# Encoder trunk: where TensorE's operands begin in SBUF, modulo 256 bytes

## The chip, the cores and the metric

One core of a Trainium2 chip runs the whole program. The metric is the device time of one execution in microseconds (us). SBUF is written here by the byte at which a tile begins in each of its 128 partitions; a tile's **residue** is that byte modulo 256.

## The reference

Two layers over 512 tokens of width 1024, and a memory of 256 tokens. Layer 0 mixes tokens by windowed attention, layer 1 by a bidirectional linear recurrence (RG-LRU); both also attend to the memory, and both end in a squared-ReLU MLP of width 4096:

```python
for l in range(DEPTH):
    h = rms_norm(x, mix_norm[l])
    kv = mem_n @ w_mem_kv[l]
    mixed, mq = attn_mixer(...) if l % 2 == 0 else lru_mixer(...)
    mo = memory_attention(mq, mk, mv)
    x = x + jnp.concatenate([mixed, mo], axis=-1) @ w_out[l]
    x = x + squared_relu_mlp(rms_norm(x, mlp_norm[l]), w_up[l], w_down[l])
return rms_norm(x, final_norm)
```

## The kernel before, in words

**Numbers.** Every product of float32 matrices is made of three matmuls in the type float32r. An operand is split into a high part (ScalarE, ACT, rounds it: `A.copy` or `A.activation`) and a low part (VectorE, DVE, subtracts), and TensorE (PE) adds high by high, high by low and low by high: `mm3`, lines 117 to 119, and in the MLPs lines 394 to 396. Each matmul has a **stationary** operand of 128 columns, which a weight load (PEld) brings in, and a **moving** operand of 256 or 512 columns, which streams past it. All data stands transposed: channels on partitions, tokens along the free dimension.

**Weights.** They come from HBM in 298 pieces of 128 x 1024 (512 KB) through tiles `raw` and are split into `wh` and `wl` (`split_w`, lines 112 and 113, outside the MLPs; `split_raw`, lines 351 and 352, in them). A tile `wh` holds eight stationary operands side by side.

**Stages, in the order of time.** The memory's keys and values of layer 0 (`ps_mk`, `ps_mv`); the memory attention (`ps_mq`, scores `sc` from `mq` and `mkh`, output `pv`); keys, values and queries (`ps_k`, `ps_v`, `ps_q`); window attention (`sc`, `pt`, `pv`); the output projection (`ps_o`, first from `om`, then from `o`, each 512 columns); MLP 0 from about 277 to 613 us; then the same for layer 1 with the recurrence (`ps_xb`, `ps_g`, `ps_gt`) in place of the window attention, and MLP 1 from 865 us to the end. Where the projections move tokens they move 512 columns (`h`, `om`, `o`, `ol`, `xh`); `ps_mk`, `ps_mv`, `ps_v` and the scores `sc` of the memory move 256.

**The MLPs** (`mlp`, line 425) cut each matrix product into 2 x 2 blocks and form it by seven block products (`seven`, line 399; `product`, line 386). Each block product is 24 matmuls that move 256 columns: `hx`, `h7` (activations of the up step) or `u7` (of the down step) move, `wh` and `wl` stand still. The last quarter of MLP 1's down step (`emit_last`, line 534) has plain products from `ul` into `ps_d`, 256 columns as well.

**What sets the order.** A scheduler orders the instructions by priority; `ahead(n)` raises it by n. The residues have no part in that.

**Where tiles lie.** Pools are stacks: those of the left side grow upward from byte 16,512 (residue 128), those with `side="right"` downward from byte 229,344. In a pool the tags lie in the order of their first tile, each tile rounded up to 32 bytes, with `bufs` of them side by side. So a pool's size shifts whatever is opened after it on its side. Lines that set residues before: the pad of 8 floats at line 73, the pools `const` (lines 77 to 82 and 613), `st` (lines 146 to 185), `mnm` and `msm` (286, 287), `nm`, `sm` and `dn` (745 to 747), `sink` (626), and the five tiles of line 827.

Of the kernel before, what the change touches and what calls it, by code (L numbers as in the profile page):

```python
# [9 lines left out]
F32 = mybir.dt.float32  # L10
# [13 lines left out]
NT = S // 128  # L24
# [8 lines left out]
C_FREQ, C_SIGN, C_HPI, C_END = 136, 137, 138, 139  # L33
# [26 lines left out]
def trunk(ctx: ExitStack, tc, xT_d, memT_d, wts_d, cols_d, ident_d, mask_d, pos_d, sink_d, outT_d, out_d, order):  # L60
# [6 lines left out]
    const = ctx.enter_context(tc.tile_pool(name="const", bufs=1))  # L67
    wp = ctx.enter_context(tc.tile_pool(name="wp", bufs=4))
    P = nc.gpsimd
    st = ctx.enter_context(tc.tile_pool(name="st", bufs=2))  # L70

    pad = ctx.enter_context(tc.tile_pool(name="pad", bufs=1, side="right"))
    pad.tile([128, 8], F32, name="pad")
    ps_m = ctx.enter_context(tc.tile_pool(name="ps_m", bufs=3, space=PSUM))
    ps_a = ctx.enter_context(tc.tile_pool(name="ps_a", bufs=2, space=PSUM))

    cols = const.tile([128, C_END], F32, name="cols")
    ident = const.tile([128, 128], F32, name="ident")
    ones = const.tile([128, 128], F32, name="ones")
    m_bc = const.tile([128, M], F32, name="m_bc")  # L80
    m_col = const.tile([128, 2], F32, name="m_col")
    xall = const.tile([128, KD, S], F32, name="xT")
    xT = [xall[:, c] for c in range(KD)]

# [79 lines left out]
    def rstd_cols(accs, n):  # L164
        nt = n // 128
        ps = ps_a.tile([128, S], F32, tag="pv", name="ps_ss", bufs=1)
        for t in range(nt):
            for i, acc in enumerate(accs):
                T.matmul(ps[:, t:t + 1], lhsT=acc[:, tok(t)], rhs=ones[:, 0:1], start=i == 0, stop=i == len(accs) - 1)
        v = st.tile([128, 4], F32, tag="v", name="v")[:, :nt]  # L170
        q = st.tile([128, 4], F32, tag="q", name="q")[:, :nt]
        r = st.tile([128, 4], F32, tag="r", name="r")[:, :nt]
        V.tensor_scalar(out=v, in0=ps[:, :nt], scalar1=1.0 / D, scalar2=EPS, op0=ALU.mult, op1=ALU.add)
        A.activation(out=q, in_=v, func=AF.Sqrt)
        V.reciprocal(out=r, in_=q)
        V.scalar_tensor_tensor(out=q, in0=r, scalar=-0.5, in1=r, op0=ALU.mult, op1=ALU.mult)
        V.tensor_tensor(out=q, in0=q, in1=v, op=ALU.mult)
        V.scalar_tensor_tensor(out=r, in0=q, scalar=1.5, in1=r, op0=ALU.add, op1=ALU.mult)
        return r
# [95 lines left out]
    def mem_attn(pool, w_in, col0, mkh, mvh, h, bc, o, bufs=2):  # L275
        for hd in range(4):
            ps = proj(load_w("s", w_in, col0 + hd * 128), h, "ps_mq")
            q = pool.tile([128, 2, S], F32R, tag="mq", name="mq", bufs=2)
            if bc is None:
                split_scaled(part(q), ps, 128.0 ** -0.5)  # L280
            else:
                qf = pool.tile([128, S], F32, tag="mqf", name="mqf", bufs=2)
                V.scalar_tensor_tensor(out=qf, in0=ps, scalar=128.0 ** -0.5, in1=bc, op0=ALU.mult, op1=ALU.mult)
                split(part(q), qf)
            p = pool.tile([128, NT, M], F32, tag="mp", name="mp", bufs=2)
            nm = pool.tile([128, NT], F32, tag="mnm", name="mnm", bufs=2)
            sm = pool.tile([128, NT], F32, tag="msm", name="msm", bufs=2)
            for g in range(2):
                sc = ps_a.tile([128, 2, M], F32, tag="sc", name="sc")
                for t2 in range(2):  # L290
                    mm3(sc[:, t2, :], part(q, tok(g * 2 + t2)), part(mkh[hd]), True, True)
                V.tensor_reduce(out=nm[:, g * 2:g * 2 + 2], in_=sc, axis=AX, op=ALU.max, negate=True)
                for t2 in range(2):
                    t = g * 2 + t2
                    A.activation(out=p[:, t, :], in_=sc[:, t2, :], func=AF.Exp, bias=nm[:, t:t + 1], scale=1.0,
                                 accum_out=sm[:, t:t + 1])
            V.reciprocal(out=sm, in_=sm)
            for t in range(NT):
                A.activation(out=p[:, t, :], in_=p[:, t, :], func=AF.Copy, scale=sm[:, t:t + 1])
            op = ps_a.tile([128, S], F32, tag="pv", name="pv", bufs=1)  # L300
            for m in range(2):
                pt = ps_a.tile([128, S], F32, tag="pt", name="pt")
                for t in range(NT):
                    T.transpose(pt[:, tok(t)], p[:, t, tok(m)], ident)
                ptr = pool.tile([128, 2, S], F32R, tag="mpt", name="mpt", bufs=2)
                split(part(ptr), pt)
                mm3(op, part(mvh[m], tok(hd)), part(ptr), m == 0, m == 1)
            split(part(o[hd]), op)
# [116 lines left out]
    def mlp(l, extra=None, extra2=None):  # L425
        hpm = tc.tile_pool(name=f"hm{l}", bufs=7, side="right")
        hm = hpm.__enter__()
        with tc.tile_pool(name=f"raws{l}", bufs=RAWS) as rp, tc.tile_pool(name=f"mlp{l}", bufs=2) as up:
            b = blocks_of(up)
            acc = st.tile([128, S], F32, tag="acc", name="acc", bufs=1)  # L430
            with ahead(AHEAD_E):
                plain = [hm.tile([128, 2, 4, 256], F32R, tag="h7", name="hx", bufs=7) for _ in range(2)]
            for c in range(KD):
                with ahead(AHEAD_E):
                    split_scaled(part(plain[c % 2], c // 2), xT[c][:, :256], col(C_MLP + 8 * l + c))
                add_square(acc, xT[c], c == 0)
# [97 lines left out]
            def emit_last():  # L534
                with tc.tile_pool(name="last", bufs=4, side="right") as lp:
                    u, b = {}, us.pop(3)
                    for n in (11, 21, 12, 22):
                        u[n] = lp.tile([128, 2, 4, 256], F32R, tag="ul", name="ul")
                        for k in range(2):
                            k = slice(2 * k, 2 * k + 2)  # L540
                            split((u[n][:, 0, k], u[n][:, 1, k]), b[n][:, k])

                    def down(w, half):
                        ps = mtile(256, "ps_d")
                        for k in range(KD):
                            mm3(ps, wcol(w, k), part(u[(11, 21)[k % 2] + half], k // 2), k == 0, k == KD - 1)
                        return ps

                    acc = st.tile([128, S], F32, tag="acc", name="acc", bufs=1)
                    for c in range(5):  # L550
                        w = load_w("s", f"w_down{l}", c * 128, 3 * 1024)
                        for half in range(2):
                            add_x(c, down(w, half), HALVES[half])
                        add_square(acc, xT[c], c == 0)
                    w = [load_w("s", f"w_down{l}", c * 128, 3 * 1024) for c in (5, 6, 7)]
                    for half in range(2):
                        cut = HALVES[half]
                        for c in (5, 6, 7):
                            add_x(c, down(w[c - 5], half), cut)
                            if half == 0 or c < 7:  # L560
                                add_square(acc[:, cut], xT[c][:, cut], False)
                        if half == 0:
                            final_first(acc, lp)
                    final_rest(acc, lp)
# [45 lines left out]


    nc.gpsimd.memset(ones, 1.0)
    warm = const.tile([128, 1], F32, name="warm")
    A.activation(out=warm, in_=ones[:, 0:1], func=AF.Sqrt)
    nc.sync.dma_start(out=cols, in_=cols_d)
    nc.scalar.dma_start(out=ident, in_=ident_d)
# [6 lines left out]
    at_a = tc.tile_pool(name="at_a", bufs=1, side="right")  # L623
    ap = at_a.__enter__()
    mask = ap.tile([128, 384], F32, name="mask")
    sink = ap.tile([128, 16], F32, name="sink")
    nsink = ap.tile([128, 16], F32, name="nsink")

    mkh, mvh = mkv_tiles(kv0)
    with tc.tile_pool(name="memp", bufs=1) as mp:  # L630
        fetched.append(fetch_w())
        raws, memH = load_mem(mp)
        fetched.append(fetch_w())
# [103 lines left out]
    def win_attn(g, pool, o):  # L737
        for n in range(NT):
# [4 lines left out]
            for ab in range(2):  # L743
                p = pool.tile([128, 4, 384], F32, tag="p", name="p", bufs=3)
                nm = pool.tile([128, 4], F32, tag="nm", name="nm", bufs=3)
                sm = pool.tile([128, 4], F32, tag="sm", name="sm", bufs=3)
                dn = pool.tile([128, 4], F32, tag="dn", name="dn", bufs=3)
                c0 = g * 8 + ab * 4
                for j in range(4):
                    sc = ps_a.tile([128, S], F32, tag="sc", name="sc")[:, :nk]  # L750
# [49 lines left out]
    def memory1():  # L800
        kv1 = mkv_pool.__enter__()
        mp = mem_pool.__enter__()
        mem1.extend([mkv_tiles(kv1), mp, fetch_mem(mp)])

    mlp(0, memory1, lambda: mem1.append(load_mem(*mem1[1:])[1]))
    (mkh, mvh), mp, _, memH = mem1
# [35 lines left out]
    V.tensor_tensor(out=ta, in0=ta, in1=sp4, op=ALU.add)  # L842
    V.tensor_scalar(out=sp4, in0=ta, scalar1=4.0, scalar2=None, op0=ALU.mult)
    V.tensor_scalar(out=sp8, in0=ta, scalar1=-8.0, scalar2=None, op0=ALU.mult)

    rt, it, tt, xcs, xhs, hs, o_l = {}, {}, {}, {}, {}, {}, {}

# [151 lines left out]
```

## Time and profile before

| | us |
|---|---|
| median of three runs (1198.85, 1205.08, 1212.76) | 1205.08 |
| the profiled execution's own time | 1205.16 |
| its span, from first to last instruction | 1203.4 |
| PE busy with matmuls | 1157.5 |
| DVE busy | 1013.7 |
| ACT busy | 767.2 |

The span and the time differ by 1.8 us, which lie around the first and last instruction. A matmul's length in the trace (0.28 us for 256 columns) runs from its start to the end of its results and overlaps the next one's; what counts for the time is the **period**, from one start to the next. A stretch of back-to-back matmuls of one form gives it: its length divided by their number, less two that had begun before the stretch and are counted in it.

### The profile page before, as it was taken

To read this page: it belongs to the slowest core of one execution; us is meant where nothing else is said; L and a number is where in the kernel's file an instruction comes from. 1 tells how busy PE (TensorE), PEld (TensorE's weight loads), DVE (VectorE), ACT (ScalarE), POOL (GpSimd) and SP (SyncE) were. 2 spreads that over 40 slices of the span, in tenths; PEclk is the share of its full clock that TensorE was granted. 3 is DMA by queue.
4 is the path that set the end of the run, shared out by engine and by line. 5 is a ranking of instruction groups with operands and counts; after the bars stand their busy time and mean duration, and the time that the engine had idled before them with its cause. 6 is when DMAs were issued, how large, how long until landed. Compare 5 with 4: busy or idle time off the path is not lost.

```text
span 1203.4 us, 20324 instructions
## 1 busy us (share of the span) xinstructions
PE 1157.5 (96%) x8084; PEld 1065.1 (89%) x8084; DVE 1013.7 (84%) x1464; ACT 767.2 (64%) x1194; POOL 53.3 (4%) x69
## 2 busy tenths in 40 slices
PE   6999999997999999999989999999969999999997
PEld 6888788886999999999988877777869999999997
DVE  6978899868988969859978679998799798896964
ACT  7685488844666565566446779983547755757632
POOL 0000000000010101010000000001001000010000
PEclk9999999999999999999989999999989999999999
DMA  7412201162476875785434122228217766687232
GB/s 247 158 54 88 88 19 36 53 209 71 136 206 159 218 210 156 191 215 162 103 121 141 53 88 88 89 104 244 71 53 193 211 180 201 163 227 210 72 106 70
DMA packets 48910, 164.44 MB, mean 137 GB/s; under 512 B 5552, under 2 KB 9008, under 8 KB 48816
## 3 DMA queue, kind: packets, MB, share of 16 engines
q1 hardware_dynamic: 39456, 130.90, 31.3%
q0 software_dynamic: 8640, 31.46, 14.5%
q8 instruction: 63, 1.03, 0.3%
q10 hardware_dynamic: 720, 0.79, 0.2%
q14 instruction: 31, 0.25, 0.1%
HBM read 161.04 MB, written 2.10 MB: 136 GB/s over the span
## 4 chain that ended last, share of the span: by engine, by line
PE 75%; DVE 17%; ACT 3%; DMA 3%; issue 2%; SPq 0%; DVEq 0%; ACTq 0%
PE ps L395 13%; PE ps L394 13%; PE ps L396 13%; DVE wl L352 3%; PE ps_o L117 3%; PE ps_o L119 3%; PE ps_o L118 3%; DMA raw<-wts 2%; DVE xT L528 2%; PE sc L752 2%; PE pt L772 1%; DVE wl L113 1%; PE pv L117 1%; PE ps_mq L118 1%; PE ps_q L119 1%
## 5 line engine op out<-in xcount | busy, mean ns | idle before, releaser
L351 ACT CAST wh<-raw 128x1024 fp32r<-128x1024 f32 x210 | 219.1, 1048 | 178.1 <-PE ps L395 120.7
L352 DVE TENSOR_TENSOR wl<-raw,wh 128x1024 fp32r<-128x1024 f32 x210 | 254.9, 1217 | 60.5 <-ACT wh L351 59.7
L394 PE MATMUL ps<-h,wh 128*128 128x256 f32 x832 | 234.3, 282 | 12.1 <-ACT h L134 12.1
L395 PE MATMUL ps<-h,wh 128*128 128x256 f32 x832 | 234.4, 282 | 6.3 <-DVE h L135 6.3
L396 PE MATMUL ps<-h,wl 128*128 128x256 f32 x832 | 233.7, 281 | 0.0
L396 PE MATMUL ps<-u,wl 128*128 128x256 f32 x784 | 218.9, 279 | 1.9 <-DVE wl L352 1.8
L394 PE MATMUL ps<-u,wh 128*128 128x256 f32 x784 | 219.3, 280 | 1.1 <-DVE xT L528 1.0
L395 PE MATMUL ps<-u,wh 128*128 128x256 f32 x784 | 218.7, 279 | 0.6 <-DVE u L135 0.6
L394 PEld LDWEIGHTS ps<-h,wh 128*128 128x128 f32 x832 | 158.7, 191 | 12.7 <-ACT h L134 12.5
L395 PEld LDWEIGHTS ps<-h,wh 128*128 128x128 f32 x832 | 158.4, 190 | 7.3 <-DVE h L135 7.3
L396 PEld LDWEIGHTS ps<-h,wl 128*128 128x128 f32 x832 | 160.2, 192 | 0.0
L396 PEld LDWEIGHTS ps<-u,wl 128*128 128x128 f32 x784 | 149.1, 190 | 2.3 <-DVE wl L352 2.3
L394 PEld LDWEIGHTS ps<-u,wh 128*128 128x128 f32 x784 | 148.0, 189 | 2.0 <-issue 1.7
L395 PEld LDWEIGHTS ps<-u,wh 128*128 128x128 f32 x784 | 147.9, 189 | 0.8 <-DVE u L135 0.8
L112 ACT CAST wh<-raw 128x1024 fp32r<-128x1024 f32 x88 | 92.0, 1047 | 62.8 <-DMA raw<-wts 32.2
L113 DVE TENSOR_TENSOR wl<-raw,wh 128x1024 fp32r<-128x1024 f32 x88 | 106.9, 1216 | 28.8 <-ACT wh L112 28.5
L328 POOL DMA_DIRECT2D raw<-wts x60 | 51.9, 865 | 1061.5 <-DMA raw<-wts 487.1
L345 DVE TENSOR_TENSOR raw<-raw 128x1024 f32<-128x1024 f32 x60 | 73.0, 1219 | 0.8
L528 DVE TENSOR_TENSOR xT<-xT,ps 128x512 f32<-128x512 f32 x98 | 65.7, 676 | 0.8 <-PE ps L396 0.8
L134 ACT CAST u<-b 128x1024 fp32r<-128x1024 f32 x42 | 43.9, 1049 | 14.3 <-PE ps L396 8.3
L135 DVE TENSOR_TENSOR u<-b,u 128x1024 fp32r<-128x1024 f32 x42 | 50.9, 1212 | 0.0
L217 DVE TENSOR_TENSOR xT<-xT,ps_o 128x512 f32<-128x512 f32 x48 | 32.6, 679 | 7.8 <-PE ps_o L119 7.5
(284 smaller groups left out, 2644.2 us busy)
## 6 DMA issues: line engine op xcount, KB each, us to landing
raw<-wts SPq DMA_DIRECT2D x238, 512.0 KB, 4.2
raw<-wts POOLq DMA_DIRECT2D x60, 512.0 KB, 7.4
mraw<-memT SPq DMA_DIRECT2D x16, 128.0 KB, 4.5
xT<-xT SPq DMA_DIRECT2D x8, 256.0 KB, 5.1
outT<-xT SPq DMA_DIRECT2D x8, 128.0 KB, 1.8
out<-fo ACTq DMA_DIRECT2D x2, 256.0 KB, 3.0
out<-fo SPq DMA_DIRECT2D x2, 256.0 KB, 3.1
posi<-pos SPq DMA_DIRECT2D x1, 256.0 KB, 5.4
```

The costliest lines, as they stand in the source:

```text
L112: A.copy(out=h, in_=raw)
L113: V.tensor_tensor(out=l, in0=raw, in1=h.bitcast(F32), op=ALU.subtract)
L117: T.matmul(out, lhsT=lhsT[0], rhs=rhs[0], start=start, stop=False)
L135: V.tensor_tensor(out=dst[1], in0=src, in1=dst[0].bitcast(F32), op=ALU.subtract)
L328: P.dma_start(out=t, in_=wts_d[fetch_n[0]], accum_op=ALU.add)
L345: V.tensor_tensor(out=a["s"], in0=a["s"], in1=a[22 if i == 6 else 12], op=ALU.add)
L351: A.copy(out=h, in_=raw)
L352: V.tensor_tensor(out=l, in0=raw, in1=h.bitcast(F32), op=ALU.subtract)
L394: T.matmul(out, lhsT=wh[:, c], rhs=t[:, 0, k], start=first, stop=False, skip_group_check=True)
L395: T.matmul(out, lhsT=wh[:, c], rhs=t[:, 1, k], start=False, stop=False, skip_group_check=True)
L396: T.matmul(out, lhsT=wl[:, c], rhs=t[:, 0, k], start=False, stop=p == 1 and k == 3, skip_group_check=True)
L528: V.tensor_tensor(out=dst, in0=dst, in1=src, op=ALU.add if n < 20 else ALU.subtract)
```

## The change

It computes nothing else, and no instruction is added or taken out: it adds tiles that nobody uses and makes small tiles wider, so that other tiles begin elsewhere. The tile `warm` moves ahead of `xT`.

```diff
-    pad.tile([128, 8], F32, name="pad")
+    pad.tile([128, 56], F32, name="pad")
...
-    cols = const.tile([128, C_END], F32, name="cols")
+    cols = const.tile([128, 160], F32, name="cols")[:, :C_END]
...
-    m_col = const.tile([128, 2], F32, name="m_col")
+    m_col = const.tile([128, 64], F32, name="m_col")[:, :2]
+    warm = const.tile([128, 64], F32, name="warm")[:, :1]
...
-        r = st.tile([128, 4], F32, tag="r", name="r")[:, :nt]
+        r = st.tile([128, 12], F32, tag="r", name="r")[:, :nt]
...
-            nm = pool.tile([128, NT], F32, tag="mnm", name="mnm", bufs=2)
-            sm = pool.tile([128, NT], F32, tag="msm", name="msm", bufs=2)
+            nm = pool.tile([128, 16], F32, tag="mnm", name="mnm", bufs=2)[:, :NT]
+            sm = pool.tile([128, 16], F32, tag="msm", name="msm", bufs=2)[:, :NT]
...
         with tc.tile_pool(name=f"raws{l}", bufs=RAWS) as rp, tc.tile_pool(name=f"mlp{l}", bufs=2) as up:
+            up.tile([128, 32], F32, tag="pad", name="pad", bufs=1)
...
                 plain = [hm.tile([128, 2, 4, 256], F32R, tag="h7", name="hx", bufs=7) for _ in range(2)]
+                hm.tile([128, 32], F32, tag="pad", name="pad", bufs=1)
...
                             split((u[n][:, 0, k], u[n][:, 1, k]), b[n][:, k])
+
+                    lp.tile([128, 32], F32, tag="pad", name="pad", bufs=1)
...
-    warm = const.tile([128, 1], F32, name="warm")
...
-    sink = ap.tile([128, 16], F32, name="sink")
+    sink = ap.tile([128, 48], F32, name="sink")[:, :16]
...
     with tc.tile_pool(name="memp", bufs=1) as mp:
+        mp.tile([128, 32], F32, tag="pad", name="pad", bufs=1)
...
                 dn = pool.tile([128, 4], F32, tag="dn", name="dn", bufs=3)
+                if n == 0 and ab == 0:
+                    pool.tile([128, 56], F32, tag="pad", name="pad", bufs=1)
...
         mem1.extend([mkv_tiles(kv1), mp, fetch_mem(mp)])
+        mp.tile([128, 32], F32, tag="pad", name="pad", bufs=1)
...
     V.tensor_scalar(out=sp8, in0=ta, scalar1=-8.0, scalar2=None, op0=ALU.mult)
+
+    lp.tile([128, 48], F32, name="pad", bufs=1)
```

Added up by the rule above, the tiles that TensorE reads have these residues:

| tiles | part in the matmul | before | after |
|---|---|---|---|
| `wh`, `wl` | stationary; moving in `ps_mv` and `ps_v` | 0 | 0 |
| `hx`, `h7`, `u7`, `ul` (both MLPs) | moving, 256 columns | 192 | 128 |
| `h`, `om`, `ol` | moving, 512 columns (`h` stationary in `ps_v`) | 192 | 0 |
| `o` (window attention) | moving, 512 columns | 64 | 0 |
| `xh` | moving, 512 columns | 0 | 0 |
| `memH` | moving, 256 columns, in `ps_mk`; stationary in `ps_mv` | 192 | 128 in layer 0, 0 in layer 1 |
| `mkh`, `k` | moving, 256 and 256 or 384 columns | 192 | 0 |
| `mq`; `q` | stationary | 192; 64 | 0 |
| `mvh`, `v` | stationary | 192 | 0 |
| `mpt`; `ptr` | moving, 512 columns | 64; 224 | 0 |

The steps from one operand to the next inside a tile (512, 1024, 2048 or 4096 bytes) are multiples of 256, so a whole tile has one residue. In layer 1's pool `memp1` the pad comes between the tiles `mraw` (then at 128) and `memH`. In the MLPs the left pools then end at byte 171,648, where the right ones begin; 1,024 bytes were free between them before.

## Rows read from the trace of the kernel before

**Rows 1.** The page's parts 1 and 4: engines' busy time, and the chain that ended last.

```profile
span 1203.4 us, 20324 instructions
PE 1157.5 (96%) x8084; PEld 1065.1 (89%) x8084; DVE 1013.7 (84%) x1464; ACT 767.2 (64%) x1194; POOL 53.3 (4%) x69
...
PE 75%; DVE 17%; ACT 3%; DMA 3%; issue 2%; SPq 0%; DVEq 0%; ACTq 0%
```

**Rows 2.** Costliest groups, shapes apart: 256-column matmuls of the MLPs; idle time stands last.

```profile
L395 PE MATMUL ps<-h,wh 128*128 128x256 f32 x832 | 234.4, 282 | 6.3 <-DVE h L135 6.3
L394 PE MATMUL ps<-h,wh 128*128 128x256 f32 x832 | 234.3, 282 | 12.1 <-ACT h L134 12.1
L396 PE MATMUL ps<-h,wl 128*128 128x256 f32 x832 | 233.7, 281 | 0.0
L394 PE MATMUL ps<-u,wh 128*128 128x256 f32 x784 | 219.3, 280 | 1.1 <-DVE xT L528 1.0
...
L117 PE MATMUL ps_d<-ul,wh 128*128 128x256 f32 x128 | 35.4, 277 | 0.0
...
L394 PE MATMUL ps<-hx,wh 128*128 128x256 f32 x64 | 18.0, 282 | 0.0
```

**Rows 3.** Stretches of the two MLPs: length, then each engine's busy time and instructions.

```profile
core 0: us, PE busy (x) PEld busy (x) DVE busy (x) ACT busy (x) POOL busy (x), PEclk, DMA share, GB/s
317.50:548.50 231.00, 231.00 (x1963) 231.00 (x1963) 193.09 (x197) 147.04 (x187) 20.72 (x24) 1.00 0.70 190
549.00:555.00 6.00, 4.18 (x22) 3.90 (x21) 6.00 (x7) 3.81 (x5) 0.00 (x0) 0.74 0.51 167
555.50:594.00 38.50, 38.02 (x333) 37.77 (x332) 38.50 (x41) 21.10 (x21) 3.45 (x4) 1.00 0.66 177
889.80:899.00 9.20, 9.20 (x80) 9.20 (x80) 8.64 (x10) 6.95 (x8) 0.00 (x0) 1.00 0.17 57
899.50:907.00 7.50, 5.07 (x30) 5.03 (x30) 7.35 (x9) 1.92 (x3) 0.00 (x0) 0.77 0.23 75
907.00:985.00 78.00, 78.00 (x691) 78.00 (x690) 70.11 (x72) 56.17 (x72) 6.91 (x8) 1.00 0.75 205
990.00:1060.00 70.00, 70.00 (x620) 70.00 (x619) 60.43 (x61) 44.65 (x54) 5.17 (x6) 1.00 0.70 195
...
1150.00:1185.00 35.00, 35.00 (x311) 35.00 (x311) 16.25 (x27) 11.43 (x18) 0.00 (x0) 1.00 0.18 61
```

**Rows 4.** Stretches of 512-column matmuls: ps_q, ps_o from o, ps_o from ol.

```profile
105.00:143.00 38.00, 38.00 (x165) 30.45 (x164) 33.66 (x53) 14.78 (x19) 0.00 (x0) 1.00 0.27 98
252.00:277.00 25.00, 25.00 (x111) 20.52 (x110) 17.66 (x26) 11.16 (x18) 3.60 (x4) 1.00 0.99 286
828.00:865.00 37.00, 37.00 (x161) 29.79 (x160) 25.64 (x37) 14.97 (x23) 1.73 (x2) 1.00 0.57 165
```

**Rows 5.** Timeline of PE, ps_g from 788.63 us: start, length, engine, line.

```profile
788.63 0.40 PE L117 MATMUL ps_g<-xh,wh 128*128 128x512 f32 x1
...
790.69 0.39 PE L117 MATMUL ps_g<-xh,wh 128*128 128x512 f32 x1
```

**Rows 6.** Timeline of PE, memory scores sc from 66.97 us: twelve in a row.

```profile
66.97 0.28 PE L117 MATMUL sc<-mkh,mq 128*128 128x256 f32 x1
...
68.27 0.28 PE L119 MATMUL sc<-mkh,mq 128*128 128x256 f32 x1
```

**Rows 7.** Timeline of PE, ps_mv of layer 1, thirteen in a row.

```profile
631.07 0.28 PE L118 MATMUL ps_mv<-wl,memH 128*128 128x256 f32 x1
...
632.43 0.28 PE L118 MATMUL ps_mv<-wl,memH 128*128 128x256 f32 x1
```

**Rows 8.** Stretch of ps_v, 256 columns.

```profile
88.10:99.40 11.30, 11.30 (x98) 11.30 (x97) 10.46 (x19) 8.07 (x16) 0.00 (x0) 1.00 0.14 47
```

**Rows 9.** Costliest groups: DVE's splits of weights, raw of L352 at residue 192, L113 at 0.

```profile
L352 DVE TENSOR_TENSOR wl<-raw,wh 128x1024 fp32r<-128x1024 f32 x210 | 254.9, 1217 | 60.5 <-ACT wh L351 59.7 <-DMA raw<-wts 0.5
...
L113 DVE TENSOR_TENSOR wl<-raw,wh 128x1024 fp32r<-128x1024 f32 x88 | 106.9, 1216 | 28.8 <-ACT wh L112 28.5
```

## The prediction

> **What bounds the kernel now.** I read the page first, then the groups by shape, then stretches of one kind of matmul. The page has PE busy for 96% of the span and 75% of the chain that ended last; DVE holds 17% of that chain [rows 1]. The idle time before the MLPs' matmuls is small: 12.1 and 6.3 us ahead of the h products and hardly any ahead of the others, against more than 200 us of busy time in each group [rows 2]. So in most of the span the time is a number of matmuls times their period.
>
> The period is not one number. Between 317.5 and 548.5 us the 256-column matmuls follow each other at 231.0 us / 1,961 = 117.8 ns. From 907 us on it is 78.0 / 689 = 113.2, then 70.0 / 618 = 113.3, and in the last products of MLP 1 35.0 / 309 = 113.3 [rows 3]. The granted clock is 1.00 (the level of 2.4 GHz) in all of these, the residues are the same (stationary 0, moving 192), and neither the group of weights nor h or u makes a difference. So there are two levels, 4.5 ns apart, and a run of matmuls stays in one of them. The level changes where PE stood idle: between 549 and 555 us it was busy for 4.18 of 6.00 us and the clock fell (mean 0.74), and between 899.5 and 907 us again (5.07 of 7.50 us, 0.77); before each the period was slow (9.2 / 78 = 117.9 ns just before the second), and after the second it was fast [rows 3]. Right after the first, at 555.5 to 594 us, DVE is busy throughout and sets the pace.
>
> The 512-column matmuls differ with the residue that moves. At 192 the period is 38.0 / 163 = 233.1 ns in `ps_q` and 37.0 / 159 = 232.7 in `ps_o` from `ol`; at 64, in `ps_o` from `o`, the same code on other tiles, it is 25.0 / 109 = 229.4 [rows 4]. At 0, in `ps_g`, nine periods take 2.06 us, 228.9 each [rows 5]. I read this as two streams of reads, the moving operand's and the next weight load's, that cost each other time depending on where each stands.
>
> **The change part by part.** No instruction is added, removed or moved to another queue, no wait is added, and the DMAs are the same in number and size. What can change is the duration of what reads or writes a tile that begins elsewhere.
>
> *DVE and ACT.* The same split of a weight takes 1,217 ns where `raw` is at residue 192 (L352) and 1,216 where it is at 0 (L113) [rows 9]. These engines' durations don't depend on it: nothing.
>
> *512 columns, moving residue 192 to 0.* Projections are 34 with 24 matmuls (816), output projections at 192 make 384: 1,200 matmuls. Ends: 0, if the residue is only a companion of something else in `ps_q`; or 233.1 less two fast 256-column periods, 226.6: 6.5 ns x 1,200 = 7.8 us. I take the row with the very residues of the change, 228.9 [rows 5], which `ps_o` at 64 supports [rows 4]: 4.2 ns. About 1,000 of the 1,200 stand in back-to-back runs as in [rows 4], where PE sets the pace (DVE is busy there for 33.66 of 38.00 us at most, so it keeps up with a PE 2% faster); the rest lie between waits, where I count nothing. 4.2 ns x 1,000 = 4.2 us less. The 192 of `ps_o` from `o` go from 64 to 0: 0.5 ns x 192 = 0.1 us, nothing.
>
> *256 columns in the MLPs, moving residue 192 to 128.* These are 2,496 with h, 2,352 with u, 192 with hx and 384 with ul [rows 2]: 5,424. No row shows a moving residue of 128. What rows show around it: residues of equal size (192 and 192, the memory's scores) take 1.30 us for eleven periods, 118.2 [rows 6]; stationary 192 with moving 0 has both levels, 12 periods in 1.36 us = 113.3 in `ps_mv` [rows 7] and 11.3 / 96 = 117.7 in `ps_v` [rows 8]. So a distance of 64 or 192 between the two allows both levels and a distance of 0 is near the slow one. Ends: all 5,424 at 118.2, or all at 113.3. Of the 5,424, 1,961 + 78 = 2,039 are shown at the slow level [rows 3]; I take the rest, 3,385, as fast. All fast: 2,039 x 4.5 = 9.2 us less. All at 118.2: 3,385 x 4.9 + 2,039 x 0.4 = 17.4 us more. I take the lower end. A distance of 128 is half of the 256 bytes, so the two streams stand as far apart as residues allow. That this leaves only the fast level is an assumption; the nearest evidence is that the slower periods above belong to distances 0, 64 and 192. What is late next: in the fast stretches DVE is busy for 70.11 of 78.00 us and 60.43 of 70.00 [rows 3] and PE still has no gap, so nothing else takes over; only in the DVE-bound 38.5 us after 555.5 us can a faster PE gain nothing, and no slow matmuls are counted there.
>
> *The other 256-column groups* (`ps_mk`, `ps_mv`, `ps_v`, the memory's scores) are short and change pairs of residues; `ps_mv` and `ps_v` together are 288 matmuls, 288 x 4.5 = 1.3 us either way. I take zero.
>
> *The full SBUF.* Left and right pools meet in the MLPs where 1,024 bytes were free. They still don't overlap, so no tile waits for another that it did not wait for. Zero.
>
> Sum: 1205.16 (the profiled execution, within 0.1 us of the median) - 4.2 - 9.2 = 1191.8 us.
>
> A rule of the Trainium skill speaks against any effect. Its page "TensorE: Matmul & The Clock Gate", Part 2, has TensorE read the moving operand and the weights through two independent ports of SBUF, so that loading the next weights takes nothing from the running matmul, with N / 2.4 + 2.5 ns between matmuls (109.2 for 256 columns, 215.8 for 512); and "SBUF — State Buffer", section Operand start alignment, asks only for a multiple of the element size. Then residues would change nothing. The trace disagrees: 229.4 against 233.1 ns at two residues [rows 4], and both are above that figure.
>
> **The rivals.**
>
> 1. *Both levels stay at 128.* The level would again be drawn where PE has stood idle, and only the 512-column part gains: 1205.2 - 4.2 = 1201.0 us, with up to 8.8 us (the long slow run, 1,961 x 4.5 ns) to either side by the draw. For it: both levels are seen at distance 64 and at 192 alike [rows 3, 7, 8], and the spread of the three runs, 13.9 us, is of the size of one such long run. Against: nothing is seen at 128.
>
> 2. *Slower: the MLPs lose the fast level.* If 128 puts the weight load and the moving operand in each other's way for good, as the equal residues do [rows 6], every MLP matmul takes about 118.2 ns: 1205.2 + 17.4 - 4.2 = 1218.4 us. It decides as soon as the MLPs' mean period rises by more than 4.2 us / 5,424 = 0.8 ns. For it: the fast level depends on how two streams interlock, and that can be lost as well as won; over half of the MLPs' matmuls are fast already. Against: even the equal residues cost hardly more than the slow level.
>
> 3. *No effect.* The 4 ns between `ps_q` and `ps_o` from `o` come from elsewhere, and the change does not do what it says: 1205.2 us. For it: the difference of levels within one pair of residues shows that something other than the residue sets 4.5 ns. Against: three separate 512-column groups order themselves by residue.
>
> The rule of two independent ports comes out as rival 3.
>
> **How the numbers follow.** Chances: forecast 0.45, rival 1 0.30, rival 2 0.15, rival 3 0.07, and 0.03 for periods below 113.3 that no row shows. Faster by over 1% means under 1193.0, slower by over 1% means over 1217.1 (about what a measurement of this kernel can tell from no change). The forecast lies 1.2 us inside the first bound and falls short of it about once in six: 0.45 x 0.83 = 0.37; rival 1 reaches it with a good draw, 0.05; the last case 0.03: faster 0.45. Rival 2 is over the upper bound half of the time, and an unlucky draw of rival 1 or more cost than 118.2 adds a little: slower 0.12. Within 1%: 0.43. The range goes from 1184 (all 512-column matmuls at 226.6 and the short groups gaining too: 1205.2 - 7.8 - 9.2 - 1.3 = 1186.9, and a little for fewer waits) to 1214 (rival 1 with its worst draw is 1209.8, and rival 2 at the slow level of 117.8 only, 3,385 x 4.5 = 15.2 us more, 1216.2; the range takes in the first and stops short of the second). The likeliest case alone would be 1187 to 1196.
>
> **What would show it.** In the profile after, stretches such as 317 to 548 us must have 113.3 ns in both MLPs, over at least 95% of their back-to-back matmuls, and no long run at 117.8. `ps_q` and `ps_o` must come down from 233 to about 229 ns. Idle time of PE must stay as it is. The prediction is wrong if long runs at 117.8 or above remain in an MLP (rivals 1 and 2, told apart by whether 113.3 is still found), if the 512-column periods stay at 233 (rival 3), or if DVE's share in the chain grows by as much as PE's falls.

## The result, and the profile after

The kernel with the change takes 1213.7 us (median of 12 runs, 1209.2 to 1217.8) against 1202.5 us before (12 runs, 1198.9 to 1212.8): the ratio is 1.008, with an interval of 1.0055 to 1.0106. It is slower by 0.8%, where 1191.8 us had been forecast. The profiled execution took 1213.68 us, 8.5 us more than the one of before.

The page of the kernel after, parts 1 and 4:

```profile
span 1211.9 us, 20324 instructions
PE 1166.9 (96%) x8084; PEld 1081.5 (89%) x8084; DVE 1015.7 (84%) x1464; ACT 767.8 (63%) x1194; POOL 53.3 (4%) x69
...
PE 75%; DVE 16%; DMA 3%; ACT 3%; issue 2%; SPq 0%; DVEq 0%; ACTq 0%
```

Against [rows 1] the number of instructions is the same and PE's busy time is 9.4 us longer; the span grew by 8.5 us, so PE's idle time did not grow. The time went into the matmuls themselves. The stretches of the kernel after, first four of the MLPs, then `ps_q`, `ps_o` from `o`, `ps_o` from `ol`, and `ps_v` (columns as in [rows 3]; line numbers are two to eleven higher after the change):

```profile
318.00:550.00 232.00, 232.00 (x1957) 232.00 (x1956) 191.78 (x195) 147.61 (x187) 20.71 (x24) 1.00 0.69 189
567.00:608.00 41.00, 41.00 (x348) 41.00 (x347) 41.00 (x48) 20.21 (x20) 1.72 (x2) 1.00 0.45 122
990.00:1060.00 70.00, 70.00 (x592) 70.00 (x592) 57.30 (x57) 42.72 (x53) 5.17 (x6) 1.00 0.67 181
1157.00:1193.00 36.00, 36.00 (x306) 36.00 (x305) 14.59 (x24) 10.39 (x17) 0.00 (x0) 1.00 0.16 57
99.00:141.50 42.50, 42.50 (x189) 35.15 (x188) 37.43 (x59) 16.68 (x23) 0.00 (x0) 1.00 0.29 100
250.00:275.00 25.00, 25.00 (x112) 20.71 (x111) 17.28 (x25) 10.72 (x18) 3.60 (x4) 1.00 0.96 289
825.00:862.00 37.00, 37.00 (x165) 30.61 (x164) 26.40 (x38) 15.36 (x24) 1.72 (x2) 1.00 0.60 168
87.10:98.60 11.50, 11.50 (x98) 11.50 (x97) 10.60 (x20) 8.29 (x16) 0.00 (x0) 1.00 0.13 46
```

In MLP 0 the period is 232.0 / 1,955 = 118.7 ns, in MLP 1 it is 70.0 / 590 = 118.6 and in its last products 36.0 / 304 = 118.4. Both levels of [rows 3] are gone from the long stretches, and what took their place is slower than either. The row of 990 us is the plainest to read: the same 70 us held 620 matmuls before and hold 592 now, at a granted clock of 1.00 both times. The 512-column matmuls became faster, and more than forecast: 42.5 / 187 = 227.3 ns in `ps_q`, 25.0 / 110 = 227.3 and 37.0 / 163 = 227.0 in `ps_o`, against 233.1, 229.4 and 232.7 [rows 4]. Length over count can be off by one matmul, which is 1 to 2 ns in stretches as short as these. From the first start to the last of the same rows of matmuls the periods are 226.8, 226.7 and 227.0 after, and 233.3, 228.9 and 233.3 before.

The sum by these rows, with the prediction's counts: 3,385 matmuls of the MLPs rose from 113.3 to 118.7 ns, 2,039 from 117.8 to 118.7: 18.3 + 1.8 = 20.1 us more. Of the 512-column matmuls 1,200 fell by about 6.5 ns, 7.8 us less, and 192 by 2.2 ns, 0.4 us less. That makes 11.9 us more, against 11.2 between the medians and 8.5 between the two profiled executions. The agreement hides two terms that are too large. Both kernels run the same 8,084 matmuls in the same order, so the start of one and the same matmul can be compared in the two traces:

| from the first matmul of a stage to that of the next, us | before | after | after less before |
|---|---|---|---|
| start of the program to MLP 0 | 277.50 | 275.54 | -1.96 |
| MLP 0 | 335.89 | 339.53 | +3.64 |
| layer 1, `ps_mk` | 17.56 | 14.31 | -3.25 |
| layer 1, from `ps_mv` to MLP 1 | 234.48 | 232.75 | -1.73 |
| MLP 1 to the end | 337.95 | 349.77 | +11.82 |

The MLPs cost 15.5 us more and not 20.1. The stages with 512 columns gave 3.7 us and not 8.2, in part because waits took up some of it: from `ps_mv` to MLP 1 PE is idle for 5.7 us after and for 3.7 before. The 3.3 us in `ps_mk` are no gain of the change: there PE waited for 2.45 us in the execution of before, and the granted clock fell (mean 0.81), while after it waited for 1.65 us and the clock stayed at 1.00. The kernel before_mlp128 below has the old residues in this stage and took 12.49 us, at 1.00. Before and after:

```profile
613.40:631.00 17.60, 15.15 (x107) 14.95 (x106) 11.89 (x21) 8.33 (x14) 0.00 (x0) 0.81 0.45 149
615.10:629.30 14.20, 12.55 (x106) 12.34 (x105) 11.66 (x21) 8.05 (x14) 0.00 (x0) 1.00 0.41 144
```

### The profile page after: what moved, and what is told of

Same layout as the page of the kernel before. It is cut to its first block, busy times and chain, and to the rows that moved or that the text cites. A ratio compares the mean times of both kernels' runs of the same rounds, so it can differ in the third digit from the quotient of the medians.

```text
span 1211.9 us, 20324 instructions
## 1 busy us (share of the span) xinstructions
PE 1166.9 (96%) x8084; PEld 1081.5 (89%) x8084; DVE 1015.7 (84%) x1464; ACT 767.8 (63%) x1194; POOL 53.3 (4%) x69
## 4 chain that ended last, share of the span: by engine, by line
PE 75%; DVE 16%; DMA 3%; ACT 3%; issue 2%; SPq 0%; DVEq 0%; ACTq 0%
PE ps L397 15%; PE ps L398 15%; PE ps L396 15%; DMA raw<-wts 2%; PE ps_o L119 2%; PE ps_o L120 2%; PE ps_o L121 2%; DVE wl L354 2%; DVE wl L115 2%; PE sc L760 2%; PE pt L780 1%; PE pv L119 1%; PE ps_d L119 1%; PE ps_mq L120 1%; PE ps_d L120 1%
## 5 line engine op out<-in xcount | busy, mean ns | idle before, releaser
L354 DVE TENSOR_TENSOR wl<-raw,wh 128x1024 fp32r<-128x1024 f32 x210 | 256.2, 1224 | 70.6 <-ACT wh L353 69.6
L396 PE MATMUL ps<-h,wh 128*128 128x256 f32 x832 | 236.7, 285 | 12.1 <-ACT h L136 12.1
L397 PE MATMUL ps<-h,wh 128*128 128x256 f32 x832 | 236.8, 285 | 6.1 <-DVE h L137 6.1
L398 PE MATMUL ps<-h,wl 128*128 128x256 f32 x832 | 236.2, 284 | 0.0
L398 PE MATMUL ps<-u,wl 128*128 128x256 f32 x784 | 221.4, 282 | 1.8 <-DVE wl L354 1.8
L396 PE MATMUL ps<-u,wh 128*128 128x256 f32 x784 | 221.6, 283 | 0.4 <-DVE xT L532 0.4
L397 PE MATMUL ps<-u,wh 128*128 128x256 f32 x784 | 221.4, 282 | 0.2 <-DVE u L137 0.2
L347 DVE TENSOR_TENSOR raw<-raw 128x1024 f32<-128x1024 f32 x60 | 73.2, 1224 | 0.8
```

The lines of the kernel that those rows point to most:

```text
L347: V.tensor_tensor(out=a["s"], in0=a["s"], in1=a[22 if i == 6 else 12], op=ALU.add)
L354: V.tensor_tensor(out=l, in0=raw, in1=h.bitcast(F32), op=ALU.subtract)
L396: T.matmul(out, lhsT=wh[:, c], rhs=t[:, 0, k], start=first, stop=False, skip_group_check=True)
L397: T.matmul(out, lhsT=wh[:, c], rhs=t[:, 1, k], start=False, stop=False, skip_group_check=True)
L398: T.matmul(out, lhsT=wl[:, c], rhs=t[:, 0, k], start=False, stop=p == 1 and k == 3, skip_group_check=True)
```

## The experiments

**The theory after the result.** What sets the period is the distance between the residue at which the moving operand begins and that of the stationary operand, and it does so separately for 256 and for 512 columns. For 512 columns 0 is best; for 256 columns the long runs at 128 have one level only, and a slow one. The rivals: the loss comes from other parts of the new layout (B), or from the moving operand's own residue (C).

**mlp192: the MLPs' part alone is undone.** The kernel after, with pads of 192 bytes on the left and 64 on the right in place of 128 each:

```diff
-            up.tile([128, 32], F32, tag="pad", name="pad", bufs=1)
+            up.tile([128, 48], F32, tag="pad", name="pad", bufs=1)
...
-                hm.tile([128, 32], F32, tag="pad", name="pad", bufs=1)
+                hm.tile([128, 16], F32, tag="pad", name="pad", bufs=1)
...
-                    lp.tile([128, 32], F32, tag="pad", name="pad", bufs=1)
+                    lp.tile([128, 16], F32, tag="pad", name="pad", bufs=1)
```

> The kernel after with one thing undone: in both MLPs the moving operands are at residue 192 again, all others as after (512 columns at 0). Theory A (the distance between the residues of the moving and the stationary operand sets the period; in the MLPs a distance of 128 allows only 118.7 ns, 192 allows 113.3 or 117.8): MLP periods of 113.3 or 117.8 in long runs, 512 columns still 226.7, time about 1202.5 - 8 = 1194.5 us, between 1188 and 1203 by which level the long runs get. Rival B (the loss comes from elsewhere in the new layout: fully packed SBUF, DVE's operations that became 0.5% longer, the other 256-column groups): the time stays above 1209.

Measured: 1194.95 us (12 runs, 1188.8 to 1201.2), as theory A had it; ratio to before 0.9924 (0.9892 to 0.9956; before took 1204.28 us here, the median of 23 runs). The left and right pools meet without a free byte here too, and only tiles of the MLPs begin elsewhere than in the kernel after, so rival B falls: the loss was the residue in the MLPs. Stretches of MLP 0, then of the end of MLP 1:

```profile
317.00:395.00 78.00, 78.00 (x690) 78.00 (x690) 71.24 (x74) 55.81 (x72) 6.90 (x8) 1.00 0.75 205
1046.00:1123.00 77.00, 77.00 (x681) 77.00 (x681) 67.39 (x71) 51.76 (x66) 6.10 (x8) 1.00 0.63 165
1123.00:1125.00 2.00, 1.82 (x16) 1.66 (x15) 2.00 (x3) 0.85 (x1) 0.00 (x0) 1.00 0.00 0
1125.00:1132.50 7.50, 7.50 (x66) 7.50 (x65) 7.42 (x11) 1.31 (x3) 0.00 (x0) 1.00 0.32 99
```

The long runs are at the fast level: 78.0 / 688 = 113.4 ns and 77.0 / 679 = 113.4. Between 1123 and 1125 us PE is idle for 0.18 us, with the clock at 1.00 throughout, and from there on the slow level holds (7.5 / 64 = 117.2). PE's timeline across that gap shows the change of level start by start:

```profile
1123.68 0.28 PE L396 MATMUL ps<-u,wh 128*128 128x256 f32 x1
1123.80 0.28 PE L397 MATMUL ps<-u,wh 128*128 128x256 f32 x1
1123.91 0.28 PE L398 MATMUL ps<-u,wl 128*128 128x256 f32 x1
1124.36 0.36 PE L396 MATMUL ps<-u,wh 128*128 128x256 f32 x1 [0.18 <-DVE xT L532]
1124.56 0.28 PE L397 MATMUL ps<-u,wh 128*128 128x256 f32 x1
1124.67 0.28 PE L398 MATMUL ps<-u,wl 128*128 128x256 f32 x1
1124.79 0.28 PE L396 MATMUL ps<-u,wh 128*128 128x256 f32 x1
```

So the level can change at a gap, and a fall of the clock is not needed for it. The spread of this kernel's runs, 12.3 us, is of the size of such changes; that they differ from one execution to the next is argued from it, because one execution of each kernel was traced.

The expected 1194.5 us was met in part by luck. It counted 8 us for the 512-column matmuls. In the two traces the stages outside the MLPs and `ps_mk` give 1.3 + 0.9 = 2.2 us of the 14.6 between them; 8.9 come from MLP 0, which ran mostly at the fast level here and mostly at the slow one in the trace of before, and 4.3 from `ps_mk`; 0.8 were lost in MLP 1.

**mlp64.** As mlp192, with 64 bytes on the left and 192 on the right:

```diff
-            up.tile([128, 32], F32, tag="pad", name="pad", bufs=1)
+            up.tile([128, 16], F32, tag="pad", name="pad", bufs=1)
...
-                hm.tile([128, 32], F32, tag="pad", name="pad", bufs=1)
+                hm.tile([128, 48], F32, tag="pad", name="pad", bufs=1)
...
-                    lp.tile([128, 32], F32, tag="pad", name="pad", bufs=1)
+                    lp.tile([128, 48], F32, tag="pad", name="pad", bufs=1)
```

> As mlp192, with the MLPs' moving operands at residue 64. Theory A: a distance of 64 behaves as one of 192 does (ps_v and ps_mv before showed 117.7 and 113.3 at that distance the other way round): 113.3 or 117.8 in long runs, time about 1194.5 us, 1188 to 1203. If only one level exists here: about 1189 us (all at 113.3) or 1209 us (all at 117.8). Rival B: above 1209.

Measured: 1209.11 us (12 runs, 1205.1 to 1211.0), ratio 1.0033 (1.0003 to 1.0064). The middle value that was expected is missed; the one for a slow level throughout is met. Two long stretches, one of each MLP:

```profile
320.00:540.00 220.00, 220.00 (x1870) 220.00 (x1870) 184.03 (x187) 142.30 (x181) 20.75 (x24) 1.00 0.74 198
910.00:1130.00 220.00, 220.00 (x1870) 220.00 (x1869) 186.92 (x189) 143.00 (x180) 19.89 (x23) 1.00 0.71 187
```

Both are at 220.0 / 1,868 = 117.8 ns. The fast level exists as well: between waits near the end of MLP 0 a row of 263 matmuls has 113.3 ns from start to start, from 563.7 us on (28.0 / 248 = 112.9 by the stretch):

```profile
565.00:593.00 28.00, 28.00 (x250) 28.00 (x249) 28.00 (x31) 15.09 (x15) 1.73 (x2) 1.00 0.62 159
```

The two runs of about 2,000 matmuls did not catch it. So 64 and 192 allow the same two levels and were not equally good in twelve runs each; why is open.

**before_mlp128.** The kernel before with one part of the change alone, 128 in the MLPs, by pads of 192 bytes on the left and 64 on the right on top of its own 192:

```diff
+            up.tile([128, 48], F32, tag="pad", name="pad", bufs=1)
             b = blocks_of(up)
...
+                hm.tile([128, 16], F32, tag="pad", name="pad", bufs=1)
...
+                    lp.tile([128, 16], F32, tag="pad", name="pad", bufs=1)
```

> The kernel before with one part of the change alone: the MLPs' moving operands at 128, everything else at its old residue. Theory A: MLP period 118.7 everywhere instead of a mean of 115.2, 5,424 x 3.5 ns = 19 us more, and the 512-column matmuls stay at 233: about 1202.5 + 19 = 1221 us, 1217 to 1225. Rival B: about as before, 1203.

Measured: 1216.56 us (4 runs), ratio 1.0106 (1.0051 to 1.0162). Its median misses the expected interval by half a microsecond, with the sign and 12.3 of the 19 us. One stretch of MLP 0, one of MLP 1, and `ps_q`:

```profile
320.00:540.00 220.00, 220.00 (x1856) 220.00 (x1856) 184.42 (x187) 142.37 (x181) 20.74 (x24) 1.00 0.73 196
910.00:1130.00 220.00, 220.00 (x1856) 220.00 (x1855) 185.65 (x187) 142.69 (x179) 19.88 (x23) 1.00 0.70 187
99.00:143.00 44.00, 44.00 (x190) 35.28 (x190) 38.76 (x61) 17.19 (x23) 0.00 (x0) 1.00 0.29 96
```

Both MLPs are at 220.0 / 1,854 = 118.7 ns, the value of the kernel after, in a layout that shares little else with it (768 bytes are free between the pools here); `ps_q` stayed at 44.0 / 188 = 234. MLP 1 to the end takes 349.8 us, as after. What is left between this kernel and the one after is the rest of the change without the two levels: 277.1 against 275.5 us up to MLP 0, and 234.5 against 232.8 from `ps_mv` to MLP 1, which makes 3.3 us in all. The two parts of the change pull in opposite directions, and the 512-column part is the small one.

**stat64: all distances of mlp192, every residue 64 higher.** This tells the distance from the residue itself (`wp` is the pool of `wh` and `wl`):

```diff
-    pad.tile([128, 56], F32, name="pad")
+    pad.tile([128, 40], F32, name="pad")
...
+    wp.tile([128, 16], F32, tag="pad", name="pad", bufs=1)
...
-            up.tile([128, 32], F32, tag="pad", name="pad", bufs=1)
+            up.tile([128, 48], F32, tag="pad", name="pad", bufs=1)
...
-                hm.tile([128, 32], F32, tag="pad", name="pad", bufs=1)
+                hm.tile([128, 16], F32, tag="pad", name="pad", bufs=1)
...
-                    lp.tile([128, 32], F32, tag="pad", name="pad", bufs=1)
+                    lp.tile([128, 16], F32, tag="pad", name="pad", bufs=1)
```

> All distances as in mlp192, but every operand 64 bytes further: stationary wh and wl at 64, the 512-column operands at 64, the MLPs' moving operands at 0. Theory A (the distance decides): as mlp192, 226.7 ns for 512 columns, 113.3 or 117.8 in the MLPs, about 1194.5 us, 1188 to 1203. Rival C (the moving operand's own residue decides): 512 columns at 64 go back to about 229 ns (+3 us), and 256 columns at 0 take 119.9 ns as ps_v did after the change: about 1220 us.

Measured: 1190.73 us (4 runs, 1188.7 to 1193.0), ratio 0.9892 (0.9841 to 0.9944). A stretch of MLP 0 and one of `ps_q`:

```profile
316.00:394.00 78.00, 78.00 (x690) 78.00 (x689) 71.25 (x73) 55.80 (x72) 6.92 (x8) 1.00 0.74 205
99.00:141.50 42.50, 42.50 (x189) 35.19 (x188) 37.39 (x60) 17.00 (x23) 0.00 (x0) 1.00 0.29 100
```

With moving operands at 0 the MLP runs at 78.0 / 688 = 113.4 ns, and `ps_q`, moving at 64, at 42.5 / 187 = 227.3, the counts of mlp192 (690) and of the kernel after (189). Rival C had wanted about 120 and 229. For this shift the distance decides, and not where the moving operand itself begins. The same distances give the same periods outside the MLPs: from start to start `ps_mk` of layer 0 takes 113.5 ns before (distance 192) and 118.8 after (128), and that of layer 1 takes 119.9 after (0).

**scanA and scanB: the other distances.** Built like mlp192, with the MLPs' residues at 224 (MLP 0) and 160 (MLP 1) in scanA, and 96 and 32 in scanB; scanB also moves layer 1's 512-column operands to 128 by a pad ahead of `h`. The pads of the MLPs, left and right, the one of the last quarter, and the one of scanB's layer 1:

```diff
-            up.tile([128, 32], F32, tag="pad", name="pad", bufs=1)
+            up.tile([128, (56, 40)[l]], F32, tag="pad", name="pad", bufs=1)    # scanB: (24, 8)
...
-                hm.tile([128, 32], F32, tag="pad", name="pad", bufs=1)
+                hm.tile([128, (8, 24)[l]], F32, tag="pad", name="pad", bufs=1)    # scanB: (40, 56)
...
-                    lp.tile([128, 32], F32, tag="pad", name="pad", bufs=1)
+                    lp.tile([128, 24], F32, tag="pad", name="pad", bufs=1)    # scanB: 56
...
     hp = h_pool.__enter__()
+    hp.tile([128, 32], F32, tag="pad", name="pad", bufs=1)    # scanB only, layer 1
```

> As mlp192, with two new residues for the MLPs' moving operands: 224 in MLP 0 and 160 in MLP 1. Theory A1 (what counts is in which block of 64 bytes an operand begins): 224 behaves as 192 (113.3 or 117.8 ns) and 160 as 128 (118.7 throughout). Theory A2 (the distance counts in finer steps): levels of their own, 224 between those of 192 and 0 (119.9), 160 between those of 128 and 192, with no run at 113.3 in at least one of them. Time about 1204 us under A1 (MLP 1 at 118.7 costs 2,568 x 4 = 10 us against mlp192).

> As mlp192, with the MLPs' moving operands at 96 in MLP 0 and 32 in MLP 1, and the 512-column operands of layer 1 at 128 (those of layer 0 stay at 0). Theory A1: 96 as 64 (mostly 117.8), 32 as 0 (119.9); A2: levels of their own. For the 512 columns at a distance of 128 the rows so far (0: 226.7, 64: 228.9, 192: 233.3) leave 227 to 233; theory A wants it different from 226.7 if the distance matters there as well, and a rival (512 columns gain from leaving 192 only) wants 226.7 to 229. Time about 1212 us, with MLP 1 at 119.9 and MLP 0 at 117.8.

Measured, one execution each beside one of before at 1208.1 us: scanA 1205.5, scanB 1212.5. MLP 0 and MLP 1 of scanA:

```profile
320.00:540.00 220.00, 220.00 (x1862) 220.00 (x1861) 183.99 (x187) 142.53 (x182) 20.76 (x24) 1.00 0.73 196
900.00:1140.00 240.00, 240.00 (x2047) 240.00 (x2047) 207.41 (x212) 156.74 (x196) 20.76 (x24) 1.00 0.67 182
```

MLP 0 and MLP 1 of scanB, and `ps_o` of its layer 1:

```profile
320.00:540.00 220.00, 220.00 (x1835) 220.00 (x1835) 183.38 (x185) 140.13 (x176) 20.71 (x24) 1.00 0.73 194
910.00:1140.00 230.00, 230.00 (x1974) 230.00 (x1973) 198.31 (x201) 152.16 (x191) 20.72 (x24) 1.00 0.70 188
828.00:866.00 38.00, 38.00 (x164) 30.57 (x164) 26.65 (x39) 15.42 (x24) 1.73 (x2) 1.00 0.58 163
```

A1 falls, A2 holds: each distance has a period of its own, also in steps of 32 bytes. The times lie near those that had been worked out with A1's periods (1204 and 1212 us), which is chance: A1's periods did not come. The rival for 512 columns, a gain from leaving 192 only, falls too: at 128 they are nearly as slow as at 192 (233.3 ns in `ps_o`, 232.3 in `ps_xb`). Together with the rows above:

| distance, bytes | 0 | 32 | 64 | 96 | 128 | 160 | 192 | 224 |
|---|---|---|---|---|---|---|---|---|
| 256 columns, ns | 119.8 | 116.6 | 113.3 or 117.8 | 120.0 | 118.7 | 117.4 | 113.4 or 117.8 | 118.3 |
| 512 columns, ns | 226.8 | | 228.9 | | 233.3 | | 233.3 | |

(256 columns: 11.5 / 96, 230 / 1,972, mlp64, 220 / 1,833, 232 / 1,955, 240 / 2,045, mlp192 and [rows 3], 220 / 1,860. 512 columns, from start to start: `ps_q` after, `ps_o` from `o` and from `ol` before, `ps_o` from `ol` in scanB, where length over count gives 38 / 162 = 234.6.) Only 64 and 192 showed the fast level for 256 columns, and only 0 the fast period for 512. The distances 32, 96, 160 and 224 rest on one layer of one execution each. A second level is not special to 64 and 192: short rows after a wait have 117.8 ns at 32 (55 matmuls from 870.8 us in scanB) and 119.9 at 128 (55 from 865.4 us in before_mlp128).

**Better than both kernels:** mlp192 and stat64 beat before by the ratios above, and their medians lie 19 and 23 us under that of the kernel after. They keep the part of the change that gains, but that part is worth about 3 us in the traces, and the lead over before is 9.3 and 13.6 us between the medians. In the traces the rest is mostly MLP 0 at the fast level (8.9 us in mlp192). Whether these two kernels get it more often than before does, at the same distance in the MLPs, and why, is not shown.

## Why the prediction was wrong

*What bounds the kernel* was right: PE's periods in the MLPs, not its waits, made the kernel slower (15.5 us more), and PE's idle time did not grow. The stretch from 555.5 us was for the most part misread as paced by DVE: PE has no gap in 29.00 us from 565 us on in the trace of before, nor in the 41.00 us from 567 us after, though DVE is busy throughout in both. DVE's splits took 1,224 ns in this profile instead of 1,217 [rows 9], but 1,219 in mlp192 and 1,218 in before_mlp128, so neither part of the layout alone lengthens them; whether the two together do is open.

*512 columns*: right in sign, and near in size by two errors against each other. I took 4.2 ns from nine periods in `ps_g` [rows 5] and kept 6.5 as the end of the range; the starts give 233.3 - 226.8 = 6.5 ns in `ps_q` and 233.3 - 227.0 = 6.3 in `ps_o`. `ps_g` was not steady in those nine: three periods take 0.70 us up to the row below, 233 each, and six take 1.36 us from there on, 226.7 each.

```profile
789.33 0.39 PE L117 MATMUL ps_g<-xh,wh 128*128 128x512 f32 x1
```

Against that, I let about 1,000 of the 1,200 matmuls gain. In layer 1 from `ps_mv` on, 2.0 us more went into waits, and 3.3 to 3.7 us reached the time in all, where 4.2 were forecast.

*256 columns in the MLPs*: this is the step that failed, the sentence "A distance of 128 is half of the 256 bytes, so the two streams stand as far apart as residues allow", and with it the choice of the lower end, 9.2 us less. The runs show no order of that kind: 128 is among the slow ones (118.7), worse than 32 (116.6), and the best two are 64 and 192. The kernel before already had one of these, by accident of its pads. The sign that the prediction had named for being wrong came: long runs above 117.8 ns in both MLPs. The term was + 20.1 us by counts and periods, and 15.5 in the two traces, in place of - 9.2.

*The rivals.* Rival 2 is what happened, in mechanism and nearly in size: the MLPs lost the fast level, at 118.7 ns where I had 118.2 from the memory's scores [rows 6]. It would have given 1218.4 us; the time was 1213.7, because the MLPs lost 15.5 us and not 17.4, and because the 3.3 us in `ps_mk` came on top, from the wait and the lower clock in the execution of before. I gave it 0.15, with the equal residues' 118.2 against it. But eleven periods do not show what equal residues cost: in long rows it is 119.8 (`ps_v` after). Rival 1 described the wrong residue: levels change at gaps as it said, but the fast one is among them at 192 and 64 (mlp192, mlp64), not at 128. Rival 3 is ruled out for this kernel: stat64 and the scans move nothing but residues, and in mlp192, stat64 and the scans the period lies between 113.4 and 120.0 ns. The rule behind rival 3 is that the two reads have independent ports of SBUF, and that loading the next weights takes nothing from the running matmul (the Trainium skill, "TensorE: Matmul & The Clock Gate", Part 2). The runs disagree with what the prediction drew from it, that residues change nothing; they do not show what the ports do.

*The range* held the median by 0.3 us, and by luck: its upper end of 1214 had been set short of rival 2, which is what happened. The direction and the chances were wrong.

## What to carry to other kernels

Where TensorE's matmuls stand back to back, measure their period in a stretch without gaps, as length over count; a change of 4% in it decided the time here and was invisible in PE's busy share (96 or 97% in all eight profiles). Where tiles begin relative to each other is then worth a small scan, for each number of moving columns by itself, since the best distance for one (0 at 512 columns) is among the worst for another (256). Don't extend a pattern of distances to one that no row shows: one run with a moved pad tells 128 from 192.

## What the hardware showed that I had not expected

- One pair of residues can hold two stable periods, 113.3 and 117.8 ns at a granted clock of 1.00, over hundreds to thousands of matmuls; at a gap of 0.18 us one changed into the other.
- One such change over a run of 1,961 matmuls is worth 8.8 us, of the size of the spread between executions of the kernel before (13.9 us over twelve). At a distance of 128, where the traced long runs have one level only, twelve executions still spread over 8.6 us, so it need not be the whole of that spread.
- For 256 columns the period is not monotonic in the distance and has steps below 64 bytes (116.6 at 32, 113.3 or 117.8 at 64, 120.0 at 96).
- What stays open is why: which reads meet where in SBUF was not observed, only that the period goes with the distance. That the second stream is the weight load's is argued from the stationary operand's residue mattering, and was not measured by taking the loads away.
